# Row sums of squares from the tiles of the transposes, in place of a second load of x

## The chip, the core and the metric

The kernel runs on one core of one Trainium2 chip. The metric is the device time of one execution in microseconds. The kernel before took 2024.49 us (median of 3 runs, 2023.68 to 2028.52). A core has five engines with a queue of instructions each, worked off in order: TensorE (PE in the profile; PEld is its weight load), VectorE (DVE), ScalarE (ACT), GpSimd (POOL) and SyncE (SP), which here only issues DMAs. Engines wait for each other by semaphores.

## What is computed

One layer of an encoder on x of 512 tokens by 2048 channels, in float32: a normalised input projection, two kinds of attention, an output projection, a SwiGLU block and a last norm. What the change touches is the first norm and the projection behind it:

```python
def rmsnorm(x, g):
    xf = x.astype(jnp.float32)
    y = xf * lax.rsqrt(jnp.mean(xf * xf, axis=-1, keepdims=True) + EPS)
    return (y * g.astype(jnp.float32)).astype(x.dtype)
...
h = rmsnorm(x, g_mix[layer])
proj = jnp.einsum('bsd,de->bse', h, w_in[layer])
qa, ka, va, qb, kb, vb = jnp.split(proj, offs, axis=-1)
```

The mean of squares of a token is a factor of its whole row, so the kernel multiplies x times the gain with the weights first, and scales the rows of the product by the reciprocal root (`r1`) when it copies them out of PSUM.

## The kernel before

**Precision.** Every float32 matmul is three matmuls (`mm3`, lines 230 to 232) of operands that are split into a rounded high part and the rest. ScalarE makes the high part by a copy (`split_hi`, lines 282 and 755), VectorE the low part by a subtraction (`split_lo`, lines 287 and 758). The split weights go to a ring of eight pairs of tiles (`tw`).

**Units.** The program is a list of units. A unit is one weight tile (or one sum or difference of weight tiles) and the matmuls that use it. The loop at the end of the function walks the units in order; for each unit n it issues loads and splits for units ahead (`prepare`: loads up to some 20 us ahead, splits some 8 to 10 us ahead by planned durations), then the unit's matmuls, then the hooks of unit n, in which all other work is placed. This fixes the order in each engine's queue when the kernel is built.

**The first chunk**, units 0 to 15: keys and values of mixer A. In unit n, `x_prep(n + 1)` takes the next 128 channels of x (`xs[k]`, four 128x128 blocks in one 128x512 tile), transposes them on TensorE (line 311), copies them out with the gain (326), makes the high part (327) and the low part (328). For pairs of channels VectorE and ScalarE also make sums and differences (`x_sums`, line 348, and `x_split`, lines 343 and 344), which the later blocks use. GpSimd stores some of them to DRAM (331). Then come the unit's twelve matmuls. At the end four tiles are copied out of PSUM (`post_plain`, line 464) and stored.

**The first column block**, 56 units of six matmuls from unit 16 on. It computes a block product with seven products instead of eight; its forms run in the order m1, m2, m7, m6, m5, m4, m3, eight units each. For m7, m6, m5, m4 and m3 VectorE first forms a sum or a difference of weight tiles in place (line 792). At the end of a form, `begin` (840) copies a bank out with the row scale, or `close` (845) adds one to it. m1, m6, m5 and m3 share a pair of banks; m5 directly follows m6 and adds onto the bank that `begin` copies out after m6. With `rows_of("m1", 0, 0, begin, 7 if first else 0)` the copy after m1 stands seven units behind its end, in unit 30.

**Homes.** Tiles of x and of the weights of these blocks lie in a queue of 20 homes of 128x512 (`stage`); from unit 21 on there are four more (`more`). A home of x is put back into the queue as soon as its transposes are issued (line 312), a home of a weight when its last split is issued. All loads stand in SP's queue in program order (`load_x`, line 133; `Raw.load`, line 259), so a load that waits for its home to be free holds all loads behind it.

**The row sums.** x is loaded a second time, by rows, in eight pieces of 128x1024 (`load_rows`, line 360), into two tiles `rows`, issued between units 10 and 25. ScalarE squares each piece and sums it along the row (`row_squares`, line 363), in units 13 to 28. In unit 29 `make_r1` adds the two halves of each row (382), and VectorE, GpSimd (a power, line 212) and VectorE again make the scales `r1`.

Of the kernel before, what the change touches and what calls it, by code (L numbers as in the profile page):

```python
# [11 lines left out]
F32 = mybir.dt.float32  # L12
BF16 = mybir.dt.bfloat16
F32R = mybir.dt.float32r
AF = mybir.ActivationFunctionType
OP = mybir.AluOpType
AX = mybir.AxisListType
PSUM = bass.MemoryType.PSUM

P = 128  # L20
S = 512
D = 2048
HD = 128
NT = S // P
# [32 lines left out]
HEAD_RATE = (1.42, 1.9)  # L57
TURN_LAG = 6
VALUE_LAG = 8
COLUMN_BLOCKS = 2  # L60


def f32(ap):
    return ap.bitcast(F32)
# [3 lines left out]
def encoder_block(ctx, tc, x, g_mix, w_in, g_q_a, g_k_a, g_out_a, g_out_b, w_out, g_ffn,  # L68
                  w_gate_up, w_down, g_final, c_ident, c_mask, c_axial, c_partial, out):
    nc = tc.nc  # L70
    cp = ctx.enter_context(tc.tile_pool(name="const", bufs=1))
    wp = ctx.enter_context(tc.tile_pool(name="wstream"))
    dp = ctx.enter_context(tc.tile_pool(name="spill", bufs=1, space=bass.MemoryType.DRAM))
    sp = ctx.enter_context(tc.tile_pool(name="slots"))
# [5 lines left out]
    def nm(base):  # L80
        counter[0] += 1
        return f"{base}_{counter[0]}"

    def slot(base, dtype=F32, shape=(P, 512)):
        return sp.tile(list(shape), dtype, tag="s", name=nm(base))
# [11 lines left out]
    def bank():  # L97
        return banks.popleft()

    def release(*tiles):  # L100
        banks.extend(tiles)
# [3 lines left out]
    def small(n=4):  # L105
        used[0] += n
        assert used[0] <= 512
        return smalls[:, used[0] - n:used[0]]

    xs = [None] * KD  # L110
    stage = wp.tile([P, 20, 512], F32, tag="stage", bufs=1, name="stage")
    homes = deque(stage[:, n] for n in range(20))
    homing = [True]
    extra_homes, retired = [], []

    def more_homes():
        more = wp.tile([P, 4, 512], F32, tag="more", bufs=1, name="more")
        extra_homes.extend(more[:, n] for n in range(4))
        homes.extend(extra_homes)

    def fewer_homes():
        kept = [h for h in homes if not any(h is e for e in extra_homes)]
        homes.clear()
        homes.extend(kept)
        retired.extend(extra_homes)

    def leave_homes():
        homing[0] = False
# [11 lines left out]
    mhalf, ones = fixed[:, P + 48:P + 64], fixed[:, P + 64:P + 65]  # L140
# [17 lines left out]
    nc.vector.memset(mhalf, -0.5)  # L158
    warm = slot("warm", BF16, (P, 1024))[:, :512]
    nc.vector.memset(warm, 0.0)  # L160
    nc.scalar.activation(slot("table")[:, :1], ones, AF.Copy)
    warm_ps = bank()

    def warm_up(n):
# [75 lines left out]
    def in_turn(tiles, n, shape, dtype, tag):  # L240
        if not tiles and homing[0]:
            whole = sp.tile([P, n] + shape[1:], dtype, tag=tag + "s", bufs=1, name=nm(tag))
            tiles.extend(whole[:, i] for i in range(n))
        if not tiles:
            tiles.extend(sp.tile(shape, dtype, tag=tag, bufs=n, name=nm(tag)) for _ in range(n))
        tiles.append(tiles.pop(0))
        return tiles[-1]
# [47 lines left out]
    def hook(n, f):  # L295
        hooks.setdefault(n, []).append(f)
# [11 lines left out]
    def x_prep(k):  # L308
        ps = bank()
        for t in range(NT):  # L310
            nc.tensor.transpose(ps[:, t * P:(t + 1) * P], xs[k][:, t, :], ident)
        homes.append(xs[k].rearrange("p t c -> p (t c)"))
        i, half = divmod(k, 2)
        if half == 0:
            xpair[i] = in_turn(pairs_turn, 3, [P, 4 * 512], F32, "xpair")
        flat = xpair[i][:, half * 1024:half * 1024 + 512]
        view = flat.rearrange("p (f c) -> p f c", c=256)
        hi, lo = (arena[half][:, 0:2, i, j] for j in range(2))
        gain = gm[:, k:k + 1]
        if k == 0:  # L320
            ps3 = ps.rearrange("p (f c) -> p f c", c=256)
            nc.scalar.activation(hi, ps3, AF.Copy, scale=gain)
            nc.vector.scalar_tensor_tensor(lo, ps3, gain, f32(hi), op0=OP.mult, op1=OP.subtract)
            nc.scalar.activation(flat, ps, AF.Copy, scale=gain)
        else:
            nc.scalar.activation(flat, ps, AF.Copy, scale=gain)
            nc.scalar.activation(hi, view, AF.Copy)
            nc.vector.tensor_tensor(lo, view, f32(hi), op=OP.subtract)
        release(ps)
        if half == 0:  # L330
            hook(k, lambda: nc.gpsimd.dma_start(ar_dram[:, i], arena[0][:, 1, i]))
        else:
            hook(k + 2, lambda: x_sums(i))
            hook(k + 3, lambda: x_split(i))

    def x_sums(i):
        a_l, a_r, s3, s2, b_l, b_r, s1, s4 = (xpair[i][:, n * 256:(n + 1) * 256] for n in range(8))
        form_sums(a_l, a_r, b_l, b_r, s1, s2, s3, s4)

    def x_split(i):  # L340
        parts = xpair[i].rearrange("p (f c) -> p f c", c=256)
        for src, dst in ((parts[:, 2:4], arena[0][:, 1:3, i]), (parts[:, 6:8], arena[1][:, 2:4, i])):
            nc.scalar.activation(dst[:, :, 0], src, AF.Copy)
            nc.vector.tensor_tensor(dst[:, :, 1], src, f32(dst[:, :, 0]), op=OP.subtract)
# [6 lines left out]
        tt(s2, s1, a_l)  # L351
        tt(s4, b_l, s2)

    ss1 = small(2 * NT)
    rows, rows_turn = {}, []

    def load_rows(n):
        rows[n] = in_turn(rows_turn, 2, [P, D // 2], F32, "rows")
        t, half = divmod(n, 2)
        nc.sync.dma_start(rows[n], x[0, t * P:(t + 1) * P, half * (D // 2):(half + 1) * (D // 2)])  # L360

    def row_squares(n):
        nc.scalar.activation(rows[n], rows[n], AF.Square, accum_out=ss1[:, n:n + 1])

    for n, at in enumerate((13, 15, 18, 20, 22, 24, 26, 28)):
        hook(at - 3, lambda n=n: load_rows(n))
        hook(at, lambda n=n: row_squares(n))

    def col_sums(src):
        ps = bank()  # L370
# [8 lines left out]

    def make_r1():  # L380
        ss = small()
        nc.vector.tensor_reduce(ss, ss1.rearrange("p (t c) -> p t c", c=2), axis=AX.X, op=OP.add)
        r1["r"] = rsqrt_mean(ss, NT, D)
        r1["rs"] = small()
        nc.vector.tensor_scalar(r1["rs"], r1["r"], HD ** -0.5, None, op0=OP.mult)

    tabs = {}

    hook(29, make_r1)
    hook(21, more_homes)  # L390

    def table_tasks():
        tasks = []
# [223 lines left out]
    def head_at(slot):  # L617
        h, i = divmod(slot, NT)
        return (heads[h], i) if 0 <= h < len(heads) else (None, i)

    def head_slot(s):
        head, i = head_at(s - TURN_LAG)
        if head:
            head.pt(i)
        head, i = head_at(s - VALUE_LAG)
        if head:
# [18 lines left out]
    def attention_tasks():  # L645
# [34 lines left out]
        for h in range(NHB):  # L680
            s = NT * (NHA + h)
            at(s + 2, light(0.1, [lambda h=h: load_vB(h)]))
            at(s + 4, light(0.4, [lambda h=h: split_vB(h)]))
        for s in range(2 * NHA * NT + VALUE_LAG + 1):
            cost = 1.5 if s < NHA * NT else 1.2 if s < 2 * NHA * NT else 0.7
# [136 lines left out]
    def in_block(names, lo):  # L822
        first = not blocks
        box = ColBlock(w_in, 0, lo, KD // 2, REREAD, "craw0" if first else "craw",
                       chain=("m1", "m2", "m7", "m6", "m5", "m4", "m3") if first else CHAIN)
        blocks.append(box)
        out = {}

        def rows_of(form, i, j, f, late=0):
            box.after(form, late, lambda: [f(form, j, 2 * i + t, t) for t in range(2)])  # L830
            if form in LAST_OF_BANK:
                box.after(form, late, lambda: box.done(form))

        def begin(form, j, row, t):
            if not ends:
                ends.extend(sp.tile([P, 2, 512], F32, tag="ends", bufs=3, name=nm("ends")) for _ in range(3))
            if t == 0:
                ends.append(ends.pop(0))
            out[j, row] = ends[-1][:, t]
            nc.scalar.activation(out[j, row], box.bank_of(form)[t], AF.Copy,  # L840
                                 scale=row_scale_of(names[j])[:, row:row + 1])

        def close(form, j, row, t):
            e = out[j, row]
            nc.vector.scalar_tensor_tensor(e, box.bank_of(form)[t], row_scale_of(names[j])[:, row:row + 1], e,
                                           op0=OP.mult, op1=OP.add)
            store(names[j], row, e)

        def only(form, j, row, t):
            begin(form, j, row, t)  # L850
            store(names[j], row, out[j, row], nc.scalar)
        rows_of("m1", 0, 0, begin, 7 if first else 0)
        rows_of("m7", 1, 1, begin)
        rows_of("m6", 1, 0, begin)
        rows_of("m2", 0, 0, close)
        rows_of("m5", 1, 1, close)
        rows_of("m4", 1, 0, close)
        rows_of("m3", 0, 1, only)
# [3 lines left out]
    def in_plain(name, lo):  # L862
# [5 lines left out]
              (("qkB2", "qkB3"), (2, 3))]  # L868
    for names, lo in groups[:COLUMN_BLOCKS]:
        in_block(names, lo)  # L870
    last = blocks[-1]
# [3 lines left out]
    last.after("m3", 0, lambda: side.extend(todo))  # L875
    last.after("m3", 0, twins.clear)
    last.after("m3", 0, leave_homes)
    last.after("m5", 0, fewer_homes)
    last.after("m3", 1, lambda: reload("qA0", qA[0]))
    last.after("m3", 2, lambda: reload("kvA", kA))  # L880
    attend = [len(units)]
    for names, lo in groups[COLUMN_BLOCKS:]:
        for name, c in zip(names, lo):
# [333 lines left out]
    first = 0  # L1217
# [6 lines left out]
    at = [0.0]  # L1224
# [135 lines left out]
```

## Time and profile before

| | |
|---|---|
| runs | 2024.49 us median, 2023.68 lowest, 2028.52 highest |
| profiled execution, first to last instruction | 2023.3 us |
| TensorE busy | 1989.5 us, 98% |
| VectorE, ScalarE, GpSimd busy | 77%, 55%, 6% |
| DMA | 394.81 MB, 195 GB/s over the span |
| mean granted TensorE clock | 0.996 of full |

The profile page gives the busy time of each engine, a picture of the span in 40 slices, the DMA queues, the chain of work that ended last, and groups of instructions with what they waited for. The trace behind it can be asked for one stretch: by engine in order of time (a timeline: start, duration, engine, line, operation, output<-inputs, and in brackets the idle time before it and what ended it), by waits (engine, line, releaser: total, times, longest), or as busy times in given windows. "x2" at the end of a row of the timeline means that two instructions are shown as one. Durations of matmuls overlap, so the distance of two starts says more than a duration.

### The profile page before, as it was taken

What the parts mean: (1) busy time and instruction counts of PE and PEld (TensorE: products, weight loads), DVE (VectorE), ACT (ScalarE), POOL (GpSimd) and SP (SyncE); (2) the same over time, 40 slices, a digit from 0 to 9 for tenths busy, and PEclk for the clock granted to TensorE, in tenths of its full rate; (3) what the DMA queues carried; (4) which work ended last, traced back from release to release, by engine and by line L of the source; (5) the groups of instructions that cost most, each with busy time, mean ns of one, the idle gap of its engine ahead of it and who ended that gap; (6) DMA issues with size and microseconds to landing.
All of it is one profiled execution on the core that took longest, in us unless ns stands there. A gap on an engine that the chain in (4) does not pass through costs nothing. (4 is left out here: it accounts for less than half of the span.)

```text
span 2023.3 us, 27380 instructions
## 1 busy us (share of the span) xinstructions
PE 1989.5 (98%) x9019; PEld 1632.9 (81%) x9019; DVE 1558.8 (77%) x2771; ACT 1112.5 (55%) x1964; POOL 125.9 (6%) x155
## 2 busy tenths in 40 slices
PE   9999999999999999999999999999999999999997
PEld 7778887887788888888888888888888887788886
DVE  6778866576754688878877878778789887977977
ACT  6655344455553565555555555545546665666656
POOL 0000100000010000000000000000000121111122
PEclk9999999999999999999999999999999999999999
DMA  9777533335343546647647558458467698768855
GB/s 293 239 251 235 185 115 103 99 111 171 98 151 133 184 167 203 239 136 266 220 163 273 186 184 285 153 192 296 133 227 267 189 248 260 196 168 270 198 128 190
DMA packets 232671, 394.81 MB, mean 195 GB/s; under 512 B 21536, under 2 KB 70480, under 8 KB 232400
## 3 DMA queue, kind: packets, MB, share of 16 engines
q1 hardware_dynamic: 206032, 330.33, 48.5%
q0 software_dynamic: 14800, 32.51, 7.9%
q10 hardware_dynamic: 11696, 30.23, 4.3%
q8 instruction: 70, 1.15, 0.2%
q14 instruction: 73, 0.60, 0.1%
HBM read 329.28 MB, written 63.70 MB: 194 GB/s over the span
## 5 line engine op out<-in xcount | busy, mean ns | idle before, releaser
L230 PE MATMUL b<-tw,arena 128*128 128x512 f32 x2136 | 838.5, 393 | 7.2 <-ACT ends L840 2.5
L231 PE MATMUL b<-tw,arena 128*128 128x512 f32 x2136 | 834.0, 390 | 5.4 <-DVE tw L758 5.1
L232 PE MATMUL b<-tw,arena 128*128 128x512 f32 x2136 | 832.8, 390 | 0.0
L755 ACT ACTIVATE tw<-raw 128x512 fp32r<-128x512 f32 x924 | 559.3, 628 | 441.2 <-DVE raw L792 286.6
L758 DVE TENSOR_TENSOR tw<-raw,tw 128x512 fp32r<-128x512 f32 x924 | 619.3, 687 | 173.1 <-ACT tw L755 170.1
L231 PEld LDWEIGHTS b<-tw,arena 128*128 128x128 f32 x2136 | 401.6, 188 | 93.3 <-DVE tw L758 12.3
L230 PEld LDWEIGHTS b<-tw,arena 128*128 128x128 f32 x2136 | 401.4, 188 | 90.7 <-ACT tw L755 3.3
L232 PEld LDWEIGHTS b<-tw,arena 128*128 128x128 f32 x2136 | 401.4, 188 | 83.9
L792 DVE TENSOR_TENSOR raw<-raw,raw 128x512 f32<-128x512 f32 x528 | 361.7, 685 | 0.8 <-DMA raw<-in_w_gate_up_dram 0.6
L230 PE MATMUL b<-w,arena 128*128 128x512 f32 x368 | 146.7, 399 | 0.0
L232 PE MATMUL b<-w,arena 128*128 128x512 f32 x368 | 144.3, 392 | 0.0
L231 PE MATMUL b<-w,arena 128*128 128x512 f32 x368 | 144.1, 392 | 0.0
L1127 POOL DMA_DIRECT2D x1d<-ev x76 | 66.4, 977 | 1157.5 <-ACT ev L1126 1156.5
L232 PEld LDWEIGHTS b<-w,arena 128*128 128x128 f32 x368 | 69.5, 189 | 15.1
L231 PEld LDWEIGHTS b<-w,arena 128*128 128x128 f32 x368 | 69.6, 189 | 13.9
L230 PEld LDWEIGHTS b<-w,arena 128*128 128x128 f32 x368 | 69.5, 189 | 13.7
L758 DVE TENSOR_TENSOR tw<-stage,tw 128x512 fp32r<-128x512 f32 x93 | 62.2, 687 | 23.5 <-ACT tw L755 23.4
L755 ACT ACTIVATE tw<-stage 128x512 fp32r<-128x512 f32 x93 | 56.5, 627 | 41.8 <-DVE stage L792 29.5
L222 DVE TENSOR_TENSOR pTl<-b,pTh 128x512 fp32r<-128x512 f32 x64 | 44.0, 688 | 36.1 <-ACT pTh L221 25.4
L287 DVE TENSOR_TENSOR w<-raw,w 128x512 fp32r<-128x512 f32 x96 | 64.7, 684 | 5.7 <-ACT ends L840 3.0
L348 DVE TENSOR_TENSOR pair<-pair 128x256 f32<-128x256 f32 x120 | 45.5, 421 | 27.3 <-ACT pair L983 21.9
L1126 ACT ACTIVATE ev<-b,smalls 128x512 f32<-128x512 f32 x76 | 49.7, 683 | 29.2 <-PE b L232 28.0
(186 smaller groups left out, 1749.2 us busy)
## 6 DMA issues: line engine op xcount, KB each, us to landing
raw<-in_w_gate_up_dram SPq DMA_DIRECT2D x616, 256.0 KB, 5.3
raw<-in_w_down_dram SPq DMA_DIRECT2D x176, 256.0 KB, 6.9
stage<-in_w_in_dram SPq DMA_DIRECT2D x114, 256.0 KB, 5.1
forms<-pair SPq DMA_DIRECT2D x22, 896.0 KB, 5.3
x1d<-ev POOLq DMA_DIRECT2D x76, 256.0 KB, 6.6
fr<-forms ACTq DMA_DIRECT2D x35, 512.0 KB, 5.5
raw<-in_w_in_dram SPq DMA_DIRECT2D x64, 256.0 KB, 4.2
raw<-in_w_out_dram SPq DMA_DIRECT2D x32, 512.0 KB, 4.8
```

What stands on the lines that cost most here:

```text
L222: nc.vector.tensor_tensor(lo, src, f32(hi), op=OP.subtract)
L230: nc.tensor.matmul(dst, ah, bh, start=start, stop=False, skip_group_check=chained)
L231: nc.tensor.matmul(dst, ah, bl, start=False, stop=False, skip_group_check=chained)
L232: nc.tensor.matmul(dst, al, bh, start=False, stop=stop, skip_group_check=chained)
L287: nc.vector.tensor_tensor(self.w[1], self.src, f32(self.w[0]), op=OP.subtract)
L348: nc.vector.tensor_tensor(out, x, y, op=op)
L755: nc.scalar.activation(self.pair[:, 0], self.src, AF.Copy)
L758: nc.vector.tensor_tensor(self.pair[:, 1], self.src, f32(self.pair[:, 0]), op=OP.subtract)
L792: nc.vector.tensor_tensor(t[dst], t[src[0]], t[src[1]], op=OP.add if form == "m6" else OP.subtract)
L1126: nc.scalar.activation(e, box.bank_of(form)[t], AF.Copy, scale=r2["r"][:, row:row + 1])
L1127: nc.gpsimd.dma_start(x1_dram[2 * cb + j, row], e, accum_op=OP.add)
```

## The change

The second load of x and its two tiles are gone. In their place, behind the copies of `x_prep(k)`, ScalarE squares the tile `xs[k]` in place, and GpSimd adds it to a running sum of squares `sq1` (128x512, the four token blocks side by side). The first square goes directly to `sq1`. Only then is the home of x put back. `make_r1` reduces `sq1` over its 128 columns for each token block, in unit 20 instead of 29. The memory of the two `rows` tiles becomes four more homes, `early`, from the start; one of them is `sq1`, and in unit 12 those that are free leave the queue. `begin` after m1 stands at m1's end, in unit 23. The first ScalarE instruction, which loads its table, writes to a small tile instead of a slot.

```diff
+EARLY_HOMES = 12
...
-    extra_homes, retired = [], []
-
-    def more_homes():
-        more = wp.tile([P, 4, 512], F32, tag="more", bufs=1, name="more")
-        extra_homes.extend(more[:, n] for n in range(4))
-        homes.extend(extra_homes)
-
-    def fewer_homes():
-        kept = [h for h in homes if not any(h is e for e in extra_homes)]
+    extra_homes, retired = {}, []
+
+    def more_homes(name, tile):
+        extra_homes[name] = [tile[:, n] for n in range(4)]
+        homes.extend(extra_homes[name])
+
+
+    def fewer_homes(name):
+        kept = [h for h in homes if not any(h is e for e in extra_homes[name])]
         homes.clear()
         homes.extend(kept)
-        retired.extend(extra_homes)
+        retired.extend(extra_homes[name])
...
-    nc.scalar.activation(slot("table")[:, :1], ones, AF.Copy)
+    nc.scalar.activation(small(1), ones, AF.Copy)
...
-        homes.append(xs[k].rearrange("p t c -> p (t c)"))
...
         release(ps)
+        row_squares(k)
...
-    ss1 = small(2 * NT)
-    rows, rows_turn = {}, []
-
-    def load_rows(n):
-        rows[n] = in_turn(rows_turn, 2, [P, D // 2], F32, "rows")
-        t, half = divmod(n, 2)
-        nc.sync.dma_start(rows[n], x[0, t * P:(t + 1) * P, half * (D // 2):(half + 1) * (D // 2)])
-
-    def row_squares(n):
-        nc.scalar.activation(rows[n], rows[n], AF.Square, accum_out=ss1[:, n:n + 1])
-
-    for n, at in enumerate((13, 15, 18, 20, 22, 24, 26, 28)):
-        hook(at - 3, lambda n=n: load_rows(n))
-        hook(at, lambda n=n: row_squares(n))
+    early = sp.tile([P, 4, 512], F32, tag="rowss", bufs=1, name="early")
+    more_homes("early", early)
+    sq1 = [homes.pop()]
+
+    def row_squares(k):
+        home = xs[k].rearrange("p t c -> p (t c)")
+        if k == 0:
+            nc.scalar.activation(sq1[0], home, AF.Square)
+        else:
+            nc.scalar.activation(home, home, AF.Square)
+            nc.gpsimd.tensor_tensor(sq1[0], sq1[0], home, op=OP.add)
+        homes.append(home)
...
-        nc.vector.tensor_reduce(ss, ss1.rearrange("p (t c) -> p t c", c=2), axis=AX.X, op=OP.add)
+        nc.vector.tensor_reduce(ss, sq1[0].rearrange("p (t c) -> p t c", t=NT), axis=AX.X, op=OP.add)
...
-    hook(29, make_r1)
-    hook(21, more_homes)
+    hook(20, make_r1)
+    hook(21, lambda: more_homes("more", wp.tile([P, 4, 512], F32, tag="more", bufs=1, name="more")))
+    hook(EARLY_HOMES, lambda: fewer_homes("early"))
...
-        rows_of("m1", 0, 0, begin, 7 if first else 0)
+        rows_of("m1", 0, 0, begin)
...
-    last.after("m5", 0, fewer_homes)
+    last.after("m5", 0, lambda: fewer_homes("more"))
```

In the queues, ScalarE's 16 squares of 128x512 stand behind the instruction of line 327 of each `x_prep` (of line 324 for the first), ahead of the weight split of that unit. GpSimd's 15 sums stand between its eight stores of line 331. VectorE's reduction stands between the low parts of units 24 and 25. SP's queue has 25 loads of weights in a row where eight pieces of x stood among them, and eleven more of SP's instructions wait on GpSimd than before. TensorE's instructions and their order are the same.

## The prediction

> **What bounds the kernel now.** I read the page first, for the busy shares, then the busy time in 100 us stretches for where TensorE isn't full, and then, in those stretches, its waits and the timelines of the five queues.
>
> ```profile
> span 2023.3 us, 27380 instructions
> PE 1989.5 (98%) x9019; PEld 1632.9 (81%) x9019; DVE 1558.8 (77%) x2771; ACT 1112.5 (55%) x1964; POOL 125.9 (6%) x155
> ...
> 0.00:100.00 100.00, 95.31 (x425) 74.22 (x426) 69.25 (x130) 67.86 (x120) 6.86 (x15) 0.98 0.82 269
> 300.00:400.00 100.00, 98.09 (x468) 80.58 (x467) 63.91 (x146) 47.32 (x101) 6.10 (x5) 0.98 0.30 95
> ```
>
> In the stretches the columns are length, then busy time (and count) of PE, PEld, DVE, ACT, POOL, then granted clock, DMA share, GB/s. TensorE is the bound nearly everywhere. The change lies in the first 112 us, and its prize is what TensorE loses there. These are the places, by the timelines of TensorE and ScalarE:
>
> ```profile
> 81.14 0.39 PE L232 MATMUL b<-tw,arena 128*128 128x512 f32 x1
> 82.87 0.49 PE L230 MATMUL b<-tw,arena 128*128 128x512 f32 x1 [1.35 <-ACT tw L755]
> 83.60 0.50 PE L231 MATMUL b<-tw,arena 128*128 128x512 f32 x1 [0.23 <-DVE tw L758]
> 84.86 0.59 PE L230 MATMUL b<-tw,arena 128*128 128x512 f32 x1
> 88.44 0.39 PE L232 MATMUL b<-tw,arena 128*128 128x512 f32 x1
> 91.66 0.50 PE L231 MATMUL b<-tw,arena 128*128 128x512 f32 x1 [0.53 <-DVE tw L758]
> 107.20 0.39 PE L230 MATMUL b<-tw,arena 128*128 128x512 f32 x1
> 107.66 0.39 PE L232 MATMUL b<-tw,arena 128*128 128x512 f32 x1
> 110.58 0.50 PE L230 MATMUL b<-tw,arena 128*128 128x512 f32 x1 [2.53 <-ACT ends L840]
> ...
> 81.15 1.06 ACT L363 ACTIVATE rows<-rows 128x1024 f32<-128x1024 f32 x1 [4.38 <-DMA rows<-in_x_dram]
> 82.21 1.13 ACT L755 ACTIVATE tw<-stage 128x512 fp32r<-128x512 f32 x2
> ...
> 80.00:84.00 4.00, 2.42 (x10) 1.48 (x9) 1.15 (x2) 2.39 (x5) 0.00 (x0) 1.00 1.05 404
> 84.00:88.00 4.00, 4.00 (x13) 2.69 (x11) 2.58 (x8) 2.07 (x5) 1.04 (x1) 0.61 0.56 189
> ```
>
> Matmuls that wait for nothing start 0.23 us apart (the two steps from 107.20 to 107.66). From 81.14 to 83.60 two starts took 2.46 instead of 0.46, so 2.0 us are lost: ScalarE sat 4.38 us behind a piece of the second load of x (L363) while the weight splits (L755) that TensorE wanted stood behind it in its queue. The DMA engines were full (1.05) just then, partly with that load. In the next stretch the granted clock is 0.61: the eight starts from 84.86 to 88.44 take 3.58 us instead of 1.84, another 1.7. At 91.66 another 0.8 goes, VectorE being late. At 110.58 a start comes 2.92 after the last, 2.7 too late.
>
> **The change, part by part.** *Removed: the second load of x.*
>
> ```profile
> rows<-in_x_dram SPq DMA_DIRECT2D x8, 512.0 KB, 6.5
> L363 ACT ACTIVATE rows<-rows 128x1024 f32<-128x1024 f32 x8 | 8.4, 1052 | 7.1 <-DMA rows<-in_x_dram 6.7 <-ACT stage L464 0.4
> SPq L360 <- ACT rows L363: 15.5, 3, 8.9
> 84.98 0.16 DVE L382 TENSOR_REDUCE smalls<-smalls 128x4 f32<-128x8 f32 x1 [0.23 <-ACT rows L363]
> 86.50 0.17 DVE L385 TENSOR_SCALAR smalls<-smalls 128x4 f32<-128x4 f32 x1 [1.16 <-POOL smalls L212]
> 109.32 0.63 ACT L755 ACTIVATE tw<-stage 128x512 fp32r<-128x512 f32 x1 [0.57 <-DVE stage L792]
> 109.86 1.25 ACT L840 ACTIVATE ends<-b,smalls 128x512 f32<-128x512 f32 x2
> ```
>
> Eight transfers of 512 KB leave, about 10 us of DMA at the 404 GB/s above; so do 8.4 us of ScalarE, and SP's own 15.5 us of waiting before it may issue them, with weight loads behind. The stall at 82 has no cause left: +2.0, and with it the slow clock, +1.7. The row scale (L382 to L385) stood in VectorE's queue at 84.98, with 1.16 us of waiting for GpSimd; it moves to unit 20, more than a dozen units ahead of the split late at 91.66: +0.8. The stop at 110.58 is structural in part: m5 adds onto the bank that L840 must copy out first. But the copy began 2.2 us after the last matmul because ScalarE stood behind a split (109.32) waiting for VectorE. VectorE forms and splits a unit in two operations of 0.6 us, TensorE multiplies it in six of 0.23, 1.37: a lead, once lost behind the 82.21 of ScalarE, grows by 0.17 a unit and no faster. With the five units of lead that the issue order allows, only the first copy's 0.7 and two handovers are left, about 1.0: +1.7.
>
> *Kept, in part:* 64 to 70 us.
>
> ```profile
> 65.34 0.50 PE L231 MATMUL b<-tw,arena 128*128 128x512 f32 x1 [0.20 <-DVE tw L758]
> 67.41 0.50 PE L231 MATMUL b<-tw,arena 128*128 128x512 f32 x1 [0.40 <-DVE tw L758]
> 69.21 0.50 PE L231 MATMUL b<-tw,arena 128*128 128x512 f32 x1 [0.15 <-DVE tw L758]
> 60.64 1.06 ACT L363 ACTIVATE rows<-rows 128x1024 f32<-128x1024 f32 x1 [0.40 <-ACT stage L464]
> 62.35 0.69 DVE L758 TENSOR_TENSOR tw<-stage,tw 128x512 fp32r<-128x512 f32 x1 [2.54 <-ACT tw L755]
> L561 DVE TENSOR_REDUCE smalls<-b 128x1 f32<-128x512 f32 x18 | 12.3, 684 | 4.6 <-PE b L232 4.5
> ```
>
> Three late splits show 0.75 of idle, and cost about 1.5 (a stop's idle understates it: the 1.35 at 82.87 is 1.5 between the starts, and the start behind it is late too). Without the L363 at 60.64 VectorE's chain from 62.35 starts 1.06 sooner, which clears the first two. But the new row scale sits in this chain, between the splits of units 24 and 25: one 128x512 reduction (0.68 by the L561 row), two small operations and GpSimd's power, 2.1 in all, so unit 25 comes some 0.65 late and unit 23 still some 0.4: +0.3 is what remains (bounds -0.5 and +1.5).
>
> *Added: 16 squares on ScalarE, 15 sums on GpSimd, one in each unit of the first chunk.*
>
> ```profile
> L602 ACT ACTIVATE sq<-b 128x512 f32<-128x512 f32 x14 | 8.4, 598 | 5.1 <-ACT oT L593 4.5 <-DMA qkB<-evqkB 0.6
> L603 POOL TENSOR_TENSOR acc<-acc,sq 128x512 f32<-128x512 f32 x14 | 18.1, 1292 | 259.0 <-ACT sq L602 221.7 <-DVE smalls L565 37.4
> 9.10:54.60 45.50, 45.50 (x229) 37.49 (x228) 33.89 (x64) 33.87 (x61) 3.75 (x7) 1.00 0.90 286
> 9.05 1.14 ACT L282 ACTIVATE tw<-stage 128x512 fp32r<-128x512 f32 x2
> 10.66 0.39 PE L231 MATMUL b<-tw,arena 128*128 128x512 f32 x1
> ```
>
> A square is 0.6 (L602), 9 us of them beside ScalarE's 33.87 in 45.5: they fit, except at the start. There two squares stand ahead of the split at 9.05; it ends near 10.75, VectorE's half 0.7 later, and the matmul of 10.66 starts at 11.5: -0.8. GpSimd has 15 x 1.29 = 19.4 and 3.75 of its own DMAs in 45 us and keeps up. A home of x now comes free behind the sum, some 3.2 us later (two activations, square, sum); three more homes cover that. Three waits on GpSimd are new: SP's loads into such homes (weight loads queue behind them), the first eviction of kvA on ScalarE (splits behind it), and VectorE's reduction, which needs the fifteenth sum; each comes 3 us or more behind its sum, so I cost them at nothing, and at a sum's 1.3 where the cover is gone. The early copy of m1 (unit 23 for 30) is 1.25 of ScalarE with five splits issued ahead, and its bank isn't wanted before m6: nothing.
>
> The price I can't read directly is what the sums do to VectorE, whose operations there all take two operands from SBUF:
>
> ```profile
> 407.10 1.29 POOL L603 TENSOR_TENSOR acc<-acc,sq 128x512 f32<-128x512 f32 x1 [24.14 <-ACT sq L602]
> 407.52 1.15 DVE L570 TENSOR_SCALAR p<-p,smalls 128x512 f32<-128x512 f32 x1
> L570 DVE TENSOR_SCALAR p<-p,smalls x64: 485/487/1151, 261.6 to 581.0; 128x512 f32<-128x512 f32 x64
> 598.35 1.40 POOL L212 TENSOR_TENSOR smalls<-smalls,fixed 128x4 f32<-128x4 f32 x1 [1.59 <-DVE smalls L210]
> 598.18 2.50 DVE L287 TENSOR_TENSOR arena<-raw,arena 128x512 fp32r<-128x512 f32 x4
> ```
>
> Beside the same sum, L570 took 1.15 instead of 0.49 and ended 0.28 behind it: it was held. The four L287 beside GpSimd's power took 0.60 each, as when alone, but that power touches four elements. So the bounds are 0 and full exclusion: 19.4 of sums against 45.5 - 33.89 = 11.6 of idle VectorE, 7.8 too much. I take 0, by the operation of VectorE's own kind (two tensors); that is the weakest choice here.
>
> The Trainium skill speaks against it: "SBUF — State Buffer", section "SBUF: two separate sides", says that VectorE and GpSimd share a port pair as an exclusive lock, and counts a VectorE operation with two SBUF inputs among those that it holds against a GpSimd operation that reads SBUF. By that rule the sum would come out near rival B. L570 agrees with a lock; no row here has a long sum beside a two-tensor operation.
>
> **The sum.** 2.0 + 1.7 + 0.8 + 1.7 + 0.3 - 0.8 = 5.7 us off a span of 2023.3. The runs shown are 2023.68, 2024.49 and 2028.52: the span lies 0.4 under the lowest, 1.2 under the median. 2023.7 - 5.7 = 2018.0, and 2018.8 from the median; I write 2018.0, since two of the three runs lie nearer the lower end.
>
> **The rivals.** *B: the sums hold VectorE, and most of the gain is given back.* For it: L570, and the 11.6 of idle against 19.4. Against: the L287 rows, and a hold may be shorter than the sum's 1.29. Price 3.4 (holds of 1.0) to 7.8: 2021.4 to 2025.8. *C: slower.* Place: units 2 to 15. Full exclusion, and TensorE's repeated stops there pull the granted clock down as at 84 us, 1.7 a time. With three such spells 7.8 + 5.1 against a gain of 5.7: 2023.7 + 7.2 = 2030.9. It decides from the point where stops bunch to some 1.6 us within 3 us, as from 82 to 84; spread evenly, 7.8 over 15 units is 0.5 a unit and would not. *D: the change doesn't do what it says:* DMA is left with weights alone, yet they still come late because homes, not bandwidth, limit SP; then only the clock and L363 are gained, 3 us: 2021. Against it: the splits at 82.21 ran the moment L363 was done, so the weights were there.
>
> **How the numbers follow.** A, the forecast, 0.54, its own range 2015.0 to 2020.5: bounds of the parts (64 to 70 us: -0.5 to +1.5; the start: 0.4 to 0.8; the stop at 110: 0.5 to 2.2; and 1.7 where a slow-clock spell such as the one in the 0.98 of 300 to 400 us goes). B 0.13, D 0.04, C 0.29. 0.3% is 6.1 us, about what a measurement can tell here: faster means below 2018.4. Of A, 0.38 lies below and 0.16 above, since its open terms lean to the larger gain (64 to 70 us by 1.2 against 0.8, the start by 0.4 against 0, the spell in 300 to 400 can go or stay); B and D are within; of C 0.28 lies beyond, 0.01 within. Faster 0.38, within 0.34, slower 0.28. The range, 2015.0 to 2030.5, leaves out the worse part of C and a better A.
>
> **What would show it.** No ScalarE wait on a DMA near 82 us, granted clock 1.00 in 84 to 88, and a stop before m5 of about 1.0: gains right. VectorE's L287, L328, L344 and L348 at 0.6 to 0.7 beside the sums, and a pair of units still 6.4 us: forecast right. If those operations swell to over 1 us and a pair takes 7.0 to 7.8, the lock was real and the forecast is wrong by that.

## The result and the profile after

| | us |
|---|---|
| kernel before, 9 runs | 2026.50 median (2023.68 to 2030.17) |
| changed kernel, 9 runs | 2021.64 median (2020.50 to 2023.34) |
| ratio, with 95% interval | 0.9981 (0.9973 to 0.9989), 3.9 us less; the medians differ by 4.9 |
| profiled executions, first to last instruction | 2023.3 and 2019.0, 4.3 less |

The change is a gain of 0.2%, within what was called no change; the forecast was 5.7 less, a ratio of 0.9972. The page of the changed kernel, and its busy time in stretches (length, then PE, PEld, DVE, ACT, POOL with counts, granted clock, DMA share, GB/s):

```profile
span 2019.0 us, 27396 instructions
PE 1988.1 (98%) x9019; PEld 1631.5 (81%) x9019; DVE 1571.4 (78%) x2771; ACT 1113.7 (55%) x1964; POOL 148.8 (7%) x170
...
0.00:100.00 100.00, 93.44 (x421) 72.31 (x422) 84.74 (x133) 70.64 (x124) 29.52 (x30) 1.00 0.72 230
80.00:84.00 4.00, 4.00 (x19) 3.33 (x18) 4.00 (x7) 1.62 (x3) 0.00 (x0) 1.00 1.02 375
84.00:88.00 4.00, 4.00 (x20) 3.30 (x19) 3.99 (x8) 1.54 (x3) 0.28 (x1) 1.00 1.03 374
300.00:400.00 100.00, 98.62 (x478) 81.23 (x478) 63.01 (x143) 48.72 (x104) 6.10 (x5) 1.00 0.31 100
```

At 80 to 88 us TensorE is now full at a clock of 1.00: that part of the gain came. Yet in the first 100 us it is less busy than before (93.44 for 95.31), while VectorE's busy time has grown from 69.25 to 84.74, although it was given next to nothing new to do (the row scale's reduction takes 0.68 instead of 0.16). TensorE's waits in the first 112 us (engine, line, releaser: total, times, longest) and its timeline tell where the time went (line numbers from 61 to some 350 are mostly one higher than before: L231 to L233 are the three matmuls, L288 is the old L287, L345 and L349 the old L344 and L348):

```profile
PE b L233 <- DVE arena L328: 3.3, 5, 1.1
...
9.48 0.39 PE L233 MATMUL b<-tw,arena 128*128 128x512 f32 x1
...
10.76 0.49 PE L231 MATMUL b<-tw,arena 128*128 128x512 f32 x1 [0.45 <-ACT tw L283]
12.15 0.50 PE L232 MATMUL b<-tw,arena 128*128 128x512 f32 x1 [0.90 <-DVE tw L288]
12.48 0.40 PE L233 MATMUL b<-tw,arena 128*128 128x512 f32 x1
...
39.07 0.40 PE L232 MATMUL b<-tw,arena 128*128 128x512 f32 x1
40.06 0.50 PE L233 MATMUL b<-tw,arena 128*128 128x512 f32 x1 [0.60 <-DVE arena L328]
40.40 0.40 PE L231 MATMUL b<-tw,arena 128*128 128x512 f32 x1
...
61.95 0.50 PE L233 MATMUL b<-tw,arena 128*128 128x512 f32 x1 [1.08 <-DVE arena L328]
...
77.57 0.50 PE L232 MATMUL b<-tw,arena 128*128 128x512 f32 x1 [0.34 <-DVE tw L758]
...
108.57 0.39 PE L233 MATMUL b<-tw,arena 128*128 128x512 f32 x1
109.06 0.50 PE L231 MATMUL b<-tw,arena 128*128 128x512 f32 x1
```

Five times, about once in a pair of units, TensorE stands before the third matmul of a tile of x until VectorE has made the low part (L328). From 39.07 to 40.06 and on to 40.40 two starts took 1.33 where 0.46 is normal, so a stop costs more than its idle: 4.7 us for the five, measured so. The start lost another 1.9 at 10.76 and 12.15: from 9.48 to 12.48 it took 3.00 us, and the same steps took 1.13 before. Of the places of before, 82, 84 to 88 and 91.66 are gone, and the stop before m5 is down to 0.36 (108.57 to 109.06, and 0.1 behind it). The three late splits of 64 to 70 (units 21 to 23) are gone but for 0.2, and a new one of 0.6 stands in unit 25, at 77.57: VectorE makes the row scale (L381 in the next rows) just ahead of that split.

Why VectorE is late is seen in its timeline and GpSimd's, at the start, over one pair of units, and at the row scale (L381):

```profile
10.74 1.96 DVE L288 TENSOR_TENSOR tw<-stage,tw 128x512 fp32r<-128x512 f32 x2 [0.35 <-ACT tw L283]
...
39.33 0.68 DVE L328 TENSOR_TENSOR arena<-xpair,arena 128x512 fp32r<-128x512 f32 x1
39.93 0.68 DVE L288 TENSOR_TENSOR tw<-stage,tw 128x512 fp32r<-128x512 f32 x1
40.54 1.28 DVE L345 TENSOR_TENSOR arena<-xpair,arena 128x512 fp32r<-128x512 f32 x2
41.74 0.68 DVE L328 TENSOR_TENSOR arena<-xpair,arena 128x512 fp32r<-128x512 f32 x1
42.34 1.77 DVE L288 TENSOR_TENSOR tw<-early,tw 128x512 fp32r<-128x512 f32 x1
44.03 2.65 DVE L349 TENSOR_TENSOR xpair<-xpair 128x256 f32<-128x256 f32 x4
46.61 0.68 DVE L328 TENSOR_TENSOR arena<-xpair,arena 128x512 fp32r<-128x512 f32 x1
...
74.69 0.68 DVE L381 TENSOR_REDUCE smalls<-early 128x4 f32<-128x512 f32 x1
...
10.27 1.28 POOL L365 TENSOR_TENSOR early<-early,stage 128x512 f32<-128x512 f32 x1 [9.81 <-ACT stage L364]
...
37.84 1.29 POOL L365 TENSOR_TENSOR early<-early,stage 128x512 f32<-128x512 f32 x1 [1.56 <-issue]
41.98 1.58 POOL L365 TENSOR_TENSOR early<-early,stage 128x512 f32<-128x512 f32 x1 [2.34 <-ACT stage L364]
45.11 1.29 POOL L365 TENSOR_TENSOR early<-early,stage 128x512 f32<-128x512 f32 x1 [1.55 <-issue]
```

In the pair of units no idle time stands in brackets on VectorE: it is busy from end to end and sets the pace, 46.61 - 39.33 = 7.28 us for a pair of units where TensorE needs 6.41. But two operations are swollen. L288 at 42.34 takes 1.77 instead of 0.68, beside GpSimd's sum from 41.98 to 43.56, and the four L349 take 2.65 instead of 1.55 beside the sum from 45.11. Each sum holds VectorE for 1.1 us, and a held operation looks busy. By the distances to the next start the holds are 1.69 - 0.60 = 1.09 and 2.58 - 1.46 = 1.12 (0.60 is the step from 39.33 to 39.93; 1.46 is that of four free L349, in a run below). VectorE's own work in the pair is so 7.28 - 2.21 = 5.07.

One landmark later on tells what of the 4.3 us belongs to the change. GpSimd makes the powers of the attention's norms; the last before 312 us, of before and of after, is the same instruction:

```profile
310.33 1.11 POOL L212 TENSOR_TENSOR smalls<-smalls,fixed 128x4 f32<-128x4 f32 x1 [6.66 <-DVE smalls L210]
```

```profile
308.85 1.11 POOL L213 TENSOR_TENSOR smalls<-smalls,fixed 128x4 f32<-128x4 f32 x1 [6.66 <-DVE smalls L211]
```

So 1.5 us were gained by then, in this pair of profiles. Another 2.1 lie between 310 and 380 us: the profile of before has a spell of low clock there (0.98 of 300 to 400 us), which stands in no other profile of this study, with or without the second load. It is not the change's. The last 0.7 of the 4.3 lies later and was not followed. The runs' 3.9 is more than 1.5; what is known of that stands with the run that takes the load alone away.

### The profile page after: what moved, and what is told of

It reads as the page before. It is cut to its first block, busy times and chain, and to the rows that moved or that the text cites. A ratio compares the mean times of both kernels' runs of the same rounds, so it can differ in the third digit from the quotient of the medians.

```text
span 2019.0 us, 27396 instructions
## 1 busy us (share of the span) xinstructions
PE 1988.1 (98%) x9019; PEld 1631.5 (81%) x9019; DVE 1571.4 (78%) x2771; ACT 1113.7 (55%) x1964; POOL 148.8 (7%) x170
## 5 line engine op out<-in xcount | busy, mean ns | idle before, releaser
L231 PE MATMUL b<-tw,arena 128*128 128x512 f32 x2136 | 838.1, 392 | 2.8 <-ACT ev L1126 2.2
L233 PE MATMUL b<-tw,arena 128*128 128x512 f32 x2136 | 833.5, 390 | 3.3 <-DVE arena L328 3.3
L233 PEld LDWEIGHTS b<-tw,arena 128*128 128x128 f32 x2136 | 401.3, 188 | 89.3 <-DVE arena L328 5.7
L231 PEld LDWEIGHTS b<-tw,arena 128*128 128x128 f32 x2136 | 401.5, 188 | 85.9 <-ACT ev L1126 2.9
L231 PE MATMUL b<-w,arena 128*128 128x512 f32 x368 | 146.1, 397 | 0.0
L233 PE MATMUL b<-w,arena 128*128 128x512 f32 x368 | 143.8, 391 | 0.0
L233 PEld LDWEIGHTS b<-w,arena 128*128 128x128 f32 x368 | 69.1, 188 | 15.0
L231 PEld LDWEIGHTS b<-w,arena 128*128 128x128 f32 x368 | 69.1, 188 | 13.5
L288 DVE TENSOR_TENSOR w<-raw,w 128x512 fp32r<-128x512 f32 x96 | 64.7, 684 | 5.6 <-ACT w L283 3.7
L349 DVE TENSOR_TENSOR pair<-pair 128x256 f32<-128x256 f32 x120 | 45.5, 420 | 27.3 <-ACT pair L983 26.2
```

The lines of the kernel that those rows point to most:

```text
L231: nc.tensor.matmul(dst, ah, bh, start=start, stop=False, skip_group_check=chained)
L233: nc.tensor.matmul(dst, al, bh, start=False, stop=stop, skip_group_check=chained)
L288: nc.vector.tensor_tensor(self.w[1], self.src, f32(self.w[0]), op=OP.subtract)
L349: nc.vector.tensor_tensor(out, x, y, op=op)
```

## The experiments

Theory 1, from these rows: a sum on GpSimd holds VectorE for about 1.1 us, and VectorE then sets the pace of the first chunk. Each run was made beside runs of the kernel before on the same chip. The ratio is the one on record; it can differ from the quotient of the two medians by up to 0.0007. "Landmark" is the start of the power above: 310.33 before, 308.85 with the change.

| run | median us | ratio (95%) | landmark |
|---|---|---|---|
| no sums | 2016.56 | 0.9956 (0.9944 to 0.9969) | 304.31 |
| sums on VectorE | 2017.19 | 0.9963 (0.9949 to 0.9976) | 304.07 |
| first squares late | 2020.17 | 0.9974 (0.9965 to 0.9984) | 308.22 |
| no early homes | 2021.09 | 0.9983 (0.9974 to 0.9992) | 308.82 |
| sums on VectorE, first squares late | 2016.67 | 0.9957 (0.9945 to 0.9970) | 304.65 |
| that, scale in unit 29 | 2017.24 | 0.9959 (0.9946 to 0.9973) | 302.57 |
| squares ahead, sums on GpSimd | 2020.67 | 0.9980 (0.9971 to 0.9989) | 307.45 |
| before, one piece of the load | 2014.80 | 0.9948 (0.9935 to 0.9960) | 303.47 |
| before + sums, early, one tile | 2025.44 | 1.0001 (0.9992 to 1.0010) | 313.39 |
| before + sums, late, two tiles | 2030.88 | 1.0028 (1.0017 to 1.0038) | 316.95 |
| before + sums, late, one tile | 2026.78 | 1.0007 (0.9998 to 1.0016) | 314.59 |
| before + sums, early, two tiles | 2029.41 | 1.0022 (1.0013 to 1.0031) | 317.64 |

### The sums taken away

```diff
             nc.scalar.activation(home, home, AF.Square)
-            nc.gpsimd.tensor_tensor(sq1[0], sq1[0], home, op=OP.add)
```

> The changed kernel without GpSimd's fifteen sums; ScalarE's squares stay where they are. The sums of squares of tiles 1 to 15 are left out, so the row scale is that of the first tile alone. Theory 1 (a sum on GpSimd holds VectorE for about 1.1 us, and VectorE then sets the pace of the first chunk): the waits of TensorE on L328 (3.3 us in five stops) are gone, a pair of units takes 6.4 us again instead of 7.27, the two L288 at 10.7 us take 1.3 instead of 1.96; 4.7 + 0.7 less than the changed kernel, about 2016 where that takes 2021.6, a ratio of 0.9955 to the kernel before. Theory 2 (the sums are harmless, ScalarE's squares make VectorE's chain late): the pair stays at 7.27, the ratio at 0.998.

Measured: 2016.56, as theory 1 said to within 0.6 us. VectorE's timeline of this run, L328 two units apart:

```profile
39.15 0.69 DVE L328 TENSOR_TENSOR arena<-xpair,arena 128x512 fp32r<-128x512 f32 x1 [0.46 <-ACT arena L327]
...
45.56 0.69 DVE L328 TENSOR_TENSOR arena<-xpair,arena 128x512 fp32r<-128x512 f32 x1 [0.47 <-ACT arena L327]
```

A pair takes 6.41 again and VectorE waits for ScalarE once more. The squares, still there, cost the pair nothing; theory 2 falls. At the start they still cost TensorE 1.0 of the 1.9.

### The sums on VectorE

```diff
-            nc.gpsimd.tensor_tensor(sq1[0], sq1[0], home, op=OP.add)
+            nc.vector.tensor_tensor(sq1[0], sq1[0], home, op=OP.add)
```

> The changed kernel with the fifteen sums on VectorE instead of GpSimd. Theory 1 (GpSimd's sum holds VectorE for 1.1 us, twice what VectorE needs to do the sum itself, 0.6): VectorE has 33.9 us of work in 45.5 before the change, 9 more fit, a pair of units takes 6.4 us, L328, L288, L345, L349 take their own 0.6 to 0.7; some 4 to 5 us less than the changed kernel, about 2017, ratio 0.996. Theory 2 (VectorE is late because of ScalarE's squares): VectorE has 0.6 a unit more to do, so the pair takes 7.3 or more and the time is 2021.6 or above, ratio 0.998 to 1.001.

Measured: 2017.19. VectorE has the whole work of the sums now, and is less in the way than when GpSimd did it:

```profile
38.97 0.69 DVE L328 TENSOR_TENSOR arena<-xpair,arena 128x512 fp32r<-128x512 f32 x1 [0.22 <-ACT arena L327]
39.58 0.68 DVE L365 TENSOR_TENSOR early<-early,stage 128x512 f32<-128x512 f32 x1
...
40.79 1.55 DVE L349 TENSOR_TENSOR xpair<-xpair 128x256 f32<-128x256 f32 x4
42.25 0.68 DVE L328 TENSOR_TENSOR arena<-xpair,arena 128x512 fp32r<-128x512 f32 x1
...
45.37 0.69 DVE L328 TENSOR_TENSOR arena<-xpair,arena 128x512 fp32r<-128x512 f32 x1
```

Its own 5.07 and two sums of 0.6 make 6.27, under TensorE's 6.41; the pair takes 6.40.

### The start

```diff
-        row_squares(k)
+        if k < 2:
+            hook(k, lambda: row_squares(k))
+        else:
+            row_squares(k)
```

> The changed kernel with the squares of the first two tiles (and their sum on GpSimd) one unit later, behind the splits of weights that TensorE waits for at 10.76 and 12.15 us. Theory 1 (the start costs some 1.5 us through two squares of 0.52 each ahead of the split, and the sum at 10.27 that holds the two L288): both waits are gone, 1.5 less than the changed kernel, 2020.1, ratio 0.9974; the stops on L328 stay. Rival (the start is paid back, since VectorE sets the pace from 29 us on and TensorE would only wait longer there): the stops on L328 grow by what the start gains, and the time stays at 2021.6, ratio 0.998.

Measured: 2020.17, what theory 1 said; the interval overlaps that of the changed kernel, so the trace has to carry it. TensorE's timeline of this run has no wait at the place, and its waits still show the five stops:

```profile
9.55 0.39 PE L231 MATMUL b<-tw,arena 128*128 128x512 f32 x1
9.78 0.40 PE L232 MATMUL b<-tw,arena 128*128 128x512 f32 x1
...
PE b L233 <- DVE arena L328: 3.4, 5, 1.1
```

The 1.9 of the start is gone and isn't waited for later. (The landmark moved by only 0.6: in this profile the matmuls of the first tile start 0.43 apart, at 7.69, 8.12, 8.54 and 8.97, which loses some 0.9. The run with both edits, below, has the same, but so has the last run of all, which lacks the edit: it is not the edit's.)

### The load alone, and the rest of the change

Seven of the eight pieces of the second load, and their squares, are left out of the kernel before; the row scale is then made of one piece and a constant.

```diff
-    for n, at in enumerate((13, 15, 18, 20, 22, 24, 26, 28)):
+    hook(13, lambda: nc.vector.memset(ss1, 1024.0))
+    for n, at in enumerate((13,)):
```

> The kernel before with seven of the eight pieces of the second load of x, and their squares on ScalarE, left out: the row scale is made of one piece and a constant. The scale stays in unit 29, the copy after m1 in unit 30, and there are no early homes. Theory 1 (the gain behind the first chunk is the removed load's): no stop at 82 (2.0), no clock of 0.61 behind it (1.7), no ScalarE square ahead of the splits of 64 to 70 us (up to 1.0), the stop before m5 from 2.7 to 0.4 as in the changed kernel (2.3); 5 to 7 less than the kernel before, ratio 0.9965 to 0.9975. Theory 2 (the order of the scale and of the copy, or the homes, bring it): the stop before m5 stays above 2, the late split near 91 us stays; some 3.7 less, ratio 0.998.

Measured: 10.5 us less than before (interval 8.1 to 13.2), above the 5 to 7 expected. Its stretch behind the old stop at 82, and TensorE before m5:

```profile
84.00:88.00 4.00, 4.00 (x19) 3.34 (x18) 4.00 (x7) 1.97 (x4) 0.00 (x0) 1.00 0.93 288
...
103.23 0.39 PE L232 MATMUL b<-tw,arena 128*128 128x512 f32 x1
103.72 0.50 PE L230 MATMUL b<-tw,arena 128*128 128x512 f32 x1
```

With the scale still in unit 29, the copy after m1 still in unit 30 and no early homes, the stops at 82 and 91 and the slow clock are gone and the stop before m5 is 0.36: all of that hangs on the load and its squares. The run takes both away and doesn't part them. By the landmark it is 6.9 us, which was expected.

The runs show more, and they do so for all thirteen kernels compared here: each stands 0.5 to 3.7 us better by its ratio than by its landmark. So the profile of before is probably one of the faster executions up to 310 us (behind that it alone has the 2.1 us of low clock); this is not shown. The clock may have a part in it. Five profiles have the full load, the stop at 82 and the stop before m5: that of before and those of the four runs below that add sums to it. A low clock follows the stop at 82 in three of them (not in the two with sums of two tiles) and the stop before m5 in four (not in that of before), as here with early sums of one tile:

```profile
112.00:116.00 4.00, 4.00 (x12) 3.13 (x13) 3.96 (x7) 2.62 (x5) 0.00 (x0) 0.64 0.99 305
```

In the other three it is 0.62, 0.80 and 0.57. None of the nine profiles without the full load has such a spell between 84 and 130 us. In a spell the matmuls start 0.43 apart, and it costs some 1.6 us. It is part of the load's price, though not in every execution.

The early homes, and the order of scale and copy, were then taken out of the changed kernel in turn.

```diff
     sq1 = [homes.pop()]
+    for _ in range(3):
+        homes.pop()
```

> The changed kernel without the three early homes for weights (the running sum keeps the fourth). Theory 1 (homes are not what limits the loads in the first chunk): as the changed kernel within 0.5 us, ratio 0.998. Rival (a home of x comes free 3 us later, behind its sum, and only the extra homes cover that): SP waits on the sums with weight loads behind it, splits of units 16 on come late, and 1 to 4 us are lost, ratio 0.9985 to 1.000.

Measured: no difference (landmark 308.82 for 308.85). SP waits some 20 us for the sums, with weight loads behind it, and nothing comes late for it:

```profile
SPq L260 <- POOL early L367: 20.0, 8, 4.0
```

Scale and copy were put back on top of the two edits above, sums on VectorE and first squares late, which were also run together without it:

```diff
-    hook(20, make_r1)
+    hook(29, make_r1)
...
-        rows_of("m1", 0, 0, begin)
+        rows_of("m1", 0, 0, begin, 7 if first else 0)
```

> The changed kernel with the sums on VectorE, and the squares and sums of the first two tiles one unit later. Theory 1 (start and sums add up): 4.4 less from the sums, as that run showed, and 1.0 to 1.5 from the start, some 2016, ratio 0.9956. Rival (with its own sums VectorE sets the pace of the first chunk, so the start's gain is waited for later): stops on L328 show, and the time stays at 2017.2, ratio 0.9963.

> The changed kernel with sums on VectorE and the first two squares late, and the row scale in unit 29 and the copy after m1 in unit 30, as in the kernel before. Theory (the removed load brings all of the gain behind the first chunk; the move of the scale to unit 20 costs VectorE's chain at 64 to 73 us some 0.4 and brings nothing): the same as with the scale in unit 20 or up to 0.5 less, ratio 0.9955 to 0.9957, and the stops of 67 to 73 us shrink from 1.3 to about 0.9. Rival (the move brought the 0.8 at 91 us and the smaller stop before m5): 1 to 3 more, ratio 0.996 to 0.997.

Measured: 2016.67 and 2017.24, the same within the intervals. The first is what theory 1 said, though no better than sums on VectorE alone by more than the intervals. The waits of TensorE on the late splits, of the one and of the other:

```profile
PE b L232 <- DVE tw L761: 0.8, 3, 0.3
```

```profile
PE b L232 <- DVE tw L761: 0.3, 1, 0.3
```

No stop at 91 us comes back with the scale in unit 29. The wait in unit 25, at 73.40 in the first of the two, is gone: it was the moved scale's, 0.6 between the starts. (The other wait that no longer shows, in unit 23, has only become too short for the view: the start at 68.69 is still 0.3 late.) The move brings nothing and costs less than the runs' times can tell.

### What a sum costs: its place, or its length

If a sum is harmful, it should be so in the kernel before, and its place may matter. The first try added sums there:

```diff
             nc.scalar.activation(flat, ps, AF.Copy, scale=gain)
             nc.scalar.activation(hi, view, AF.Copy)
+            nc.gpsimd.tensor_tensor(xpair[i][:, half * 1024 + 512:half * 1024 + 1024], flat, flat, op=OP.add)
```

> The kernel before, second load of x and all, with one more GpSimd sum of 128x512 in each of units 0 to 14, on data that nothing reads (the copy of x with the gain, added to itself). No wait of another engine hangs on it that is not long served. Theory 1 (the lock): L287, L328, L344, L348 swell by about 1.1 us a sum, a pair of units goes from 6.4 towards 7.3, and TensorE stops on L328; 3 to 5 us more than the kernel before, ratio 1.0015 to 1.0025, more if the stops bring a lower granted clock. Theory 2 (sums harmless): the pair stays 6.4, ratio 1.000.

Measured: 1.0001, a miss for theory 1 by its number. The holds were there, but the pair took 6.65 only (L329 at 35.86 and 42.51), and I put that down to the place: the sum starts at L326's end, when VectorE still waits for L327. Two runs were made on that, one with the changed kernel's squares (and so its sums) ahead of the copies, one with sums in the kernel before at the later place.

```diff
+    squared = [homes.pop(), homes.pop()]
...
     def x_prep(k):
+        if k > 1:
+            row_squares(k)
         ps = bank()
...
-            nc.scalar.activation(home, home, AF.Square)
-            nc.gpsimd.tensor_tensor(sq1[0], sq1[0], home, op=OP.add)
+            nc.scalar.activation(squared[k % 2], home, AF.Square)
+            nc.gpsimd.tensor_tensor(sq1[0], sq1[0], squared[k % 2], op=OP.add)
```

> The changed kernel with GpSimd's sums kept, but each square from the third tile on ahead of the copies of its own transposes (L326, L327), into two tiles of its own, so that GpSimd's sum falls where VectorE waits for L327; the first two squares one unit late, as before. Theory (a sum costs what its hold takes beyond VectorE's idle time at that place: the 3.3 us of stops on L328 come from sums that start when VectorE's run of operations starts): a pair of units about 6.65, as with the added sums in the kernel before, one or no stop on L328; 3 to 4 less than the run with late squares alone, about 2016.5, ratio 0.9956 to 0.9963. Rival (the hold costs VectorE its 1.1 us wherever the sum falls): the stops on L328 stay, pair of 7.27, ratio 0.9974.

```diff
             nc.scalar.activation(hi, view, AF.Copy)
+            idle = xpair[i][:, half * 1024 + 512:half * 1024 + 1024].rearrange("p (f c) -> p f c", c=256)
+            nc.gpsimd.tensor_tensor(idle, view, f32(hi), op=OP.add)
```

> The kernel before with one more GpSimd sum of 128x512 in each of units 0 to 14, as in the earlier run of that kind, but of two different tiles and behind the high part (L327) where VectorE's run of operations starts, not behind the copy 0.7 earlier. Theory (place and length of the hold decide): a sum takes 1.3 and holds VectorE for 1.1 behind its L328 operation; a pair of units takes about 7.2 instead of 6.4, TensorE stops on L328 for some 4 us in all; ratio 1.001 to 1.002 (the earlier run 1.0001). Rival (in the changed kernel it was the squares on ScalarE together with the sums, not the sums): pair of 6.65, ratio 1.000.

Measured: the squares ahead brought nothing, 0.9980 and a pair of 7.28 (L330 at 37.97 and 45.25), near what its rival said; TensorE's stops on the low part shrank, from 3.4 to 1.7 of idle, but the time did not. A better place does not help. The sums in the kernel before now cost 5.7 us, with a pair of 7.26 (40.91 and 48.17). The two kernels with added sums differed in a second thing, the operands: one tile added to itself, or two tiles. The last two runs cross place and operands.

```diff
+            nc.gpsimd.tensor_tensor(idle, f32(hi), f32(hi), op=OP.add)
```

> The kernel before with an added GpSimd sum in each of units 0 to 14, at the later place (behind the high part, L327), but of one tile with itself. Two added-sum runs differed in place and in operands: early place and one tile with itself gave 1.04 us a sum and a pair of 6.65, late place and two tiles 1.36 and 7.28. Theory length (VectorE's own work in a pair of units is 5.07 us by the distances of its starts, and each of the two sums adds its hold, 1.1 for two tiles, 0.8 for one): pair 6.65, ratio 1.000 to 1.001. Theory place (a sum at the start of VectorE's run of operations costs more than one in its idle time): pair about 7.28, ratio 1.002 to 1.003.

```diff
+            last = f32(arena[1 - half][:, 0:2, (k - 1) // 2, 0])
+            nc.gpsimd.tensor_tensor(idle, view, last, op=OP.add)
```

> The kernel before with an added GpSimd sum in each of units 0 to 14, at the early place (behind L326), of two different tiles. Theory length: pair 5.07 + 2 x 1.1 = 7.27, as late and with two tiles, TensorE stops on L328, ratio 1.002 to 1.003. Theory place: pair about 6.65, as early and with one tile, ratio 1.000 to 1.001.

VectorE's timelines of both, a pair of units each (L330 and L331 are the L328 of before), late with one tile first, then early with two:

```profile
40.02 1.52 DVE L330 TENSOR_TENSOR arena<-xpair,arena 128x512 fp32r<-128x512 f32 x1
41.46 0.68 DVE L287 TENSOR_TENSOR tw<-stage,tw 128x512 fp32r<-128x512 f32 x1
42.07 2.26 DVE L350 TENSOR_TENSOR xpair<-xpair 128x256 f32<-128x256 f32 x4
44.25 0.68 DVE L330 TENSOR_TENSOR arena<-xpair,arena 128x512 fp32r<-128x512 f32 x1
...
46.66 0.68 DVE L330 TENSOR_TENSOR arena<-xpair,arena 128x512 fp32r<-128x512 f32 x1
```

```profile
41.09 1.77 DVE L331 TENSOR_TENSOR arena<-xpair,arena 128x512 fp32r<-128x512 f32 x1
42.79 0.68 DVE L287 TENSOR_TENSOR tw<-stage,tw 128x512 fp32r<-128x512 f32 x1
43.39 2.64 DVE L351 TENSOR_TENSOR xpair<-xpair 128x256 f32<-128x256 f32 x4
45.94 0.69 DVE L331 TENSOR_TENSOR arena<-xpair,arena 128x512 fp32r<-128x512 f32 x1
...
48.36 1.77 DVE L331 TENSOR_TENSOR arena<-xpair,arena 128x512 fp32r<-128x512 f32 x1
```

46.66 - 40.02 = 6.64 late with one tile, 48.36 - 41.09 = 7.27 early with two, beside 6.65 early with one and 7.26 late with two: the operands decide, not the place. A sum of one tile holds VectorE 0.84 and 0.72 in this pair (1.44 - 0.60 and 2.18 - 1.46), a sum of two tiles 1.1 each time, and 5.07 plus the two holds gives the pair in both. VectorE is saturated there, so a hold has no idle time to fall into, wherever the sum starts.

## Why the prediction was wrong

The failing step is one sentence: of the bounds 0 and full exclusion for what the sums do to VectorE, "I take 0, by the operation of VectorE's own kind (two tensors)". The row behind it was L287 beside a power on 128x4 elements, a GpSimd operation of another length; L570, which was held, lay beside the very sum that the change adds, and should have decided. What the runs showed in place of the 0 is a hold of 1.1 us of VectorE by each sum. The rival B had the mechanism and the price, 3.4 to 7.8; measured are 4.7 in the five stops and 0.8 at the start, less some 0.8 for two splits that come late only without the sums. By the ratios with and without sums (0.9981 and 0.9956) it is 5.1.

The Trainium skill, "SBUF — State Buffer", section "SBUF: two separate sides", stated the lock, and every run here with sums on GpSimd agrees with it. It speaks of the whole instruction: the hold measured is shorter, 1.1 of a sum of 1.29.

Point by point, in the profiled executions:

| step | predicted | measured |
|---|---|---|
| stall at 82 us | +2.0 | +2.1 |
| clock at 84 to 88 us | +1.7 | +1.7 |
| late split at 91.66 | +0.8 | +0.8, and without the moved scale too |
| stop before m5 | +1.7 | +2.4 |
| splits of 64 to 70 us | +0.3 | +0.7 |
| start | -0.8 | -1.9 |
| sums on VectorE | 0 | -4.7 |
| sum | 5.7 | 1.1; the landmark says 1.5 |

Of the 0.4 between the last two numbers, 0.3 is that TensorE was that much ahead before the first stop (9.48 for 9.76), which is not the change's. The runs' 3.9 is nearer to the forecast than 1.5, but the forecast was worked out from the profile of before, and against that profile the change brought 1.5.

- **Stall, clock, late split.** Shown by the run with one piece of the load. That the slow clock stood behind the stall in the profile of before, and so could be won back whole, is in part luck: with the full load it did so in three of five profiles. The reason given for 91.66 (the scale's waiting stood in VectorE's queue) is not enough: with the load gone and the scale left in unit 29 the split is not late. Whether the two together made it late was not tried.
- **Stop before m5.** Mis-sized: with ScalarE free, L840 copies the first bank while TensorE still multiplies into the second (it begins at 108.31, and the last matmul of m6 at 108.57), which the estimate of 1.0 left out; 0.36 remain.
- **64 to 70 us.** The part on the moved scale was right: unit 25 comes 0.6 late, forecast 0.65. The part on the load was not. Taking L363 away cleared unit 21 alone: in every run without the full load and without sums on GpSimd, units 22 and 23 are late, by some 0.6 and 0.4. In the changed kernel they are not, but for 0.2, so that gain goes with the sums' delay of the first chunk; that splits got ahead while TensorE was held up is my reading.
- **Start.** Two squares ahead of the split were seen, and cost 1.0. But the sum at 10.27 also held the two L288 behind it, 1.96 for 1.29; with sums gone that part goes, with squares late all of it.
- **Waits on GpSimd costed at nothing.** Right for SP (20 us of waiting that nobody feels). Rival D fell with the two runs without the early homes, of the changed kernel and of the kernel before. Rival C's mechanism did not come: stops of 0.4 to 1.1 us of idle, one in 7.3 us, left the clock at 1.00.

The version with sums on VectorE and the first two squares late leaves nothing out and beats both kernels: 2016.67 us, 0.4% under the kernel before. The kernel before without seven of the eight pieces, which leaves most of the row sums out, takes 2014.80.

## What to carry to other kernels

Before moving elementwise work to an idle GpSimd, add its time to VectorE's in that stage, as if VectorE did it, where VectorE works on two tensors as here: two sums of 1.1 on top of 5.07 us of own work exceed TensorE's pace of 6.41, and two sums of 0.6 on VectorE itself do not. Look for the hold in the durations, not in the waits: a VectorE operation of 1.77 us beside others of 0.68 of the same shape is a wait that the profile counts as busy. And take a bound from the row whose other engine does the same work, not from the one whose own operation looks alike.

## What was not expected of the hardware

GpSimd adds a 128x512 tile to itself in 1.04 us and two different tiles in 1.28 to 1.39, where no VectorE operation is in the way at the start, and holds VectorE for about 0.3 less in the first case; why was not tried. A sum that comes in the middle of a VectorE operation lasts longer itself (1.58 from 41.98, for 1.29), so GpSimd seems to wait for the end of that one operation and then goes ahead of the next. A stop of about 2.5 us of idle before m5 was followed by a granted clock of 0.57 to 0.80 in four of five profiles, the shorter stop at 82 in three of the same five; a row of stops of 0.4 to 1.1, one in some 7 us, never was.
